# Two one-row tiles of their own for the streamed conditioning rows, in place of the eighth 4 KB tile

## The chip, the cores and the metric

The kernel runs on one core of one Trainium2 chip. The metric is the device time of one execution in microseconds (us). The profile comes from one execution; its engines are PE (TensorE matmuls), PEld (TensorE weight loads, which overlap PE), DVE (VectorE), ACT (ScalarE), POOL (GpSimd) and SP (SyncE, which here only issues DMAs). L301 means line 301 of the kernel's file.

## What is computed

One layer of an encoder on x of 1024 tokens by 1024 channels, all in float32, conditioned on one vector c of 1024 entries:

```python
c_act = silu(c)
mod = c_act @ w_ada + b_ada                       # 6 x 1024 conditioning values
sh1, sc1, gt1, sh2, sc2, gt2 = split(mod, 6)
h = rms_norm(x, g_norm1) * (1 + sc1) + sh1
qa, ka, va, qb, kb, vb, gates = split(h @ w_in, ...)
o_a = neighbourhood_attention(norm(qa), norm(ka), va, rpb)          # 8 heads of 64
o_b = merge of 3 dilated window attentions on norm+rotary(qb, kb), vb   # 3 x 4 heads of 64
gate_a, gate_b = split(sigmoid(gates + b_gate))
x = x + gt1 * ((gate_a * (o_a @ w_proj_a) + gate_b * (o_b @ w_proj_b)) @ w_o)
h2 = rms_norm(x, g_norm2) * (1 + sc2) + sh2
a, up = split(h2 @ w_ffn_in)
x = x + gt2 * ((silu(a) * up) @ w_ffn_out)
```

sc1 and sh1 are needed at the very start. The other four, 4096 values, are first read after the attention, and it is their computation that the change touches.

## The kernel before, in words

**Precision.** Every matmul operand is split into a high and a low part (whi and wlo, made by `wsplit`, L118 on ACT and L119 on POOL or DVE), and each product is three matmuls.

**Stages.** First h is made (to about 48 us). Then a loop `for n in range(6, 92)` runs ten attention units `u` (two heads each) of eight token tiles `t`: the projection of the current unit (`proj_chunk`, L312, eight chunks per n), the normalisation of its result (`proj_post`, L326 to L366, the small tiles ss, ry, rv, rz and qn), the turning of q and k (`qk_turns`, L377, L399 to L402), and the attention of the unit before it (scores L476 or L543, softmax L490 to L494 or L553 to L555, turns L502 or L568, products with v L517 or L588). After u = 9 the loop goes on with the gates (`gate_pre`, L712). Then come the rest of the gates (`gate_prod`, L731), the merge, the output projection, and the feed-forward layer, which a fast block scheme runs as seven products in place of eight.

**The order of the work.** The instructions of PE are issued in the order in which the code is written. For ACT, DVE, POOL and SP that holds to the end of the first stage; from then on a list scheduler orders them when the kernel is built, from the priority of the code's order and from durations and transfer times that it assumes. On the chip each engine's list is fixed and runs in order: an instruction that waits holds up all behind it on its engine. SP is one such list, for loads and stores alike. A tile that takes a buffer can be written only when the tile that had the buffer has been read for the last time, and the scheduler places its load accordingly.

**The conditioning rows.** The 4096 values are made on DVE, beside the loop over n. A step `ada_step()` (one in each n from 8 on with t < 7, and from u = 9 on in every n; 64 in all) takes one [128, 512] block of w_ada, multiplies it by one column of c_act and adds it to the accumulator acc (L299 for the first of eight, L301 for the others). After eight steps PE sums acc over the partitions (L271, in `ada_row`), DVE adds the bias (L275) and SP stores the row. acc has one buffer. The blocks (tile name wa in the profile) come in pairs: one DMA (L283) loads two of them, 512 KB, into a big tile; at each even step the pair of that step and the next pair are asked for.

**The big tiles.** The tag `big` has eight buffers (`NBIG = 8`) of 4 KB in each partition. Besides the pairs of conditioning blocks it holds: in the first stage the landing tiles (seven, `NLAND = 7`, read by L789), then the v of each unit (loaded at L362 to L366 for units 2 to 9), two tiles (hi, lo) for each of the eight mixes of h (`t_piece`, tile tp, L751 to L761), two tables of biases (rb, L424) for each of the last four units, the accumulators of the dilated merge (oacc), the gates' results (gsig, L718, L719) and two tiles for each of two weight mixes (w1m, L766 to L772). When the loop is over, this pool is released and its place taken by the tiles of the next stage, among them tg (L1051), which L731 reads.

Of the kernel before, what the change touches and what calls it, by code (L numbers as in the profile page):

```python
# [10 lines left out]
F32 = mybir.dt.float32  # L11
# [32 lines left out]
def hybrid_layer(ctx: ExitStack, tc: tile.TileContext, x, colp, wada1, wada2, bada2, wqkv, wg, wpa, wpb,  # L44
                 wo, w1, w2, hgain, ropeg, rope, rbias, bmask, g2r, out):
    nc = tc.nc

    def pool(name, side, **kw):
        return tc.alloc_tile_pool(name=name, bufs=1, side=side, reuse_waits="tile", **kw)
# [93 lines left out]
    ap_ = pool("attn", "right")  # L143
# [2 lines left out]
    nc.vector.memset(c32, 0.0)  # L146
    nc.vector.tensor_copy(c32[:, :, 0], cact)

    NBIG, NLAND = 8, 7

    def big(name, shape=None, dtype=F32):
        return ap_.tile(shape or wide, dtype, tag="big", bufs=NBIG, name=name)
# [1 line left out]
    yT = [ap_.tile([128, 4, S], F32, tag="qk", bufs=2, name="yT") for _ in range(2)]  # L154
    land = [big("land") for _ in range(NLAND)]
    for tag, n, bufs in (("bm", 512, 1), ("p", 512, 4), ("qn", 256, 7), ("rtab", 512, 1), ("acc2", 512, 1), ("pT", 512, 4),
                         ("stg", 512, 3), ("vs", 128, 2), ("ra", 64, 2), ("rb", 64, 2)):
        ap_.tile([128, n], F32, tag=tag, bufs=bufs, name="place")
    seq = [0]

# [106 lines left out]
    ada_acc = {}  # L267

    def ada_row(c):
        pm = bank("t")  # L270
        nc.tensor.matmul(pm[0:1, :], ones, ada_acc[c], start=True, stop=True)  # L271
        row = wp.tile([1, 512], F32, tag="raw", bufs=NRAW, name="row")
        br = wp.tile([1, 512], F32, tag="raw", bufs=NRAW, name="brow")
        nc.sync.dma_start(br, bada2[:, c * 512:(c + 1) * 512])
        nc.vector.tensor_add(row, pm[0:1, :], br)  # L275
        nc.sync.dma_start(mod_d[c * 512:(c + 1) * 512].rearrange("(o n) -> o n", o=1), row)

    def ada_load(i):

        if i < 64 and i not in ada_acc.setdefault("w", {}):  # L280
            c, kk = divmod(i, 8)
            ada_acc["w"][i] = big("wa2", [128, 2, 512])
            nc.sync.dma_start(ada_acc["w"][i], wada2[c, :, kk:kk + 2, :])  # L283

    def ada_step():
        i = ada_state["i"]
        ada_state["i"] += 1
        c, kk = divmod(i, 8)
        if kk == 0 and c > 0:
            ada_row(c - 1)  # L290
        if i >= 64:
            return
        if kk % 2 == 0:
            ada_load(i)
            ada_load(i + 2)
        wa = ada_acc["w"][i - kk % 2][:, kk % 2, :]
        if kk == 0:
            ada_acc[c] = ap_.tile([128, 512], F32, tag="acc2", bufs=1, name="acc2")
            nc.vector.tensor_scalar(ada_acc[c], wa, cact[:, 0:1], None, op0=ALU.mult)  # L299
        else:  # L300
            nc.vector.scalar_tensor_tensor(ada_acc[c], wa, cact[:, kk:kk + 1], ada_acc[c],  # L301
                                           op0=ALU.mult, op1=ALU.add)
# [619 lines left out]
    for n in range(6, 92):  # L922
# [78 lines left out]
        if n >= 8 and (t != 7 or u > 8) and ada_state["i"] < 65:  # L1001
            ada_step()
# [663 lines left out]
```

## Time and profile before

| | before |
|---|---|
| median of 3 runs | 1508.83 us (1507.0 to 1510.0) |
| the profiled execution: its time / its span | 1508.52 us / 1506.7 us |
| busy share of the span: PE, DVE, ACT, POOL | 99%, 72%, 44%, 36% |
| DMA packets, bytes | 150637, 241.65 MB |

The span goes from the first instruction to the last. Busy shares are averages over stages that differ; since PE is busy nearly throughout, what counts is where it is not. A row of the waits names an instruction, what it waited for, the total in us, how often, and the longest wait. A row of the timeline begins with the start in us and the duration in us, then engine, line, operation, tiles (out<-in), shapes and count; in square brackets stands the idle time of the engine just before and what ended it. SPq marks DMA issues by SP.

### The profile page before, as it was taken

How to read it: one execution, taken by the hardware profiler on the slowest of the kernel's cores; microseconds unless marked ns; L12 is line 12 of the kernel's file. 1: busy time of each engine (PE TensorE's matmuls, PEld its weight loads, DVE VectorE, ACT ScalarE, POOL GpSimd, SP SyncE). 2: the span in 40 equal slices, each digit the busy share in tenths (PEclk: the TensorE clock that was granted, in tenths of full speed). 3: DMA queues.
4: the chain of work that ended last, by engine and by line, in shares of the span. 5: the costliest groups of instructions: out<-in, count | busy, mean ns of one | idle time of the engine just before them, and what ended most of it. 6: DMA issues, size and time to landing. Idle time of an engine off the chain costs nothing. (4 is left out here: it accounts for less than half of the span.)

```text
span 1506.7 us, 24201 instructions
## 1 busy us (share of the span) xinstructions
PE 1485.7 (99%) x8156; PEld 1265.1 (84%) x8156; DVE 1090.2 (72%) x2265; ACT 668.2 (44%) x1691; POOL 535.1 (36%) x540
## 2 busy tenths in 40 slices
PE   9999999999999999999999999999999999999998
PEld 7998989998888877788888888888888888887886
DVE  6867767767889845367675597788767777599468
ACT  5555655555645554246432354233223323354442
POOL 0432332321100040002352301676767776104464
PEclk9999999999999999999999999999999999999999
DMA  9625445645245164824553225345433334898342
GB/s 373 236 85 179 144 132 162 196 139 166 61 131 168 45 197 143 327 85 128 161 195 137 90 90 181 126 127 181 155 125 109 108 106 144 278 372 281 98 153 100
DMA packets 150637, 241.65 MB, mean 160 GB/s; under 512 B 26464, under 2 KB 69088, under 8 KB 149744
## 3 DMA queue, kind: packets, MB, share of 16 engines
q1 hardware_dynamic: 131936, 226.45, 45.7%
q10 hardware_dynamic: 18576, 13.64, 2.8%
q8 instruction: 65, 1.06, 0.3%
q14 instruction: 60, 0.49, 0.1%
HBM read 179.89 MB, written 60.15 MB: 159 GB/s over the span
## 5 line engine op out<-in xcount | busy, mean ns | idle before, releaser
L119 POOL TENSOR_TENSOR wlo<-raw,whi 128x512 fp32r<-128x512 f32 (+2 forms) x133 | 172.9, 1314 | 461.7 <-ACT whi L118 287.0
L118 ACT ACTIVATE whi<-raw 128x512 fp32r<-128x512 f32 (+1 forms) x348 | 203.6, 599 | 252.4 <-PE ps_s L1501 42.3
L312 PE MATMUL ps_d<-whi,hT 128*128 128x384 f32 x1152 | 310.8, 341 | 0.0
L119 DVE TENSOR_TENSOR wlo<-raw,whi 128x512 fp32r<-128x512 f32 (+1 forms) x215 | 183.6, 867 | 76.8 <-ACT whi L118 72.4
L312 PEld LDWEIGHTS ps_d<-whi,hT 128*128 128x128 f32 x1152 | 209.9, 188 | 5.2 <-ACT vs L350 3.5
L312 PE MATMUL ps_d<-wlo,hT 128*128 128x384 f32 x576 | 193.6, 336 | 2.9 <-DVE wlo L119 2.7
L312 PEld LDWEIGHTS ps_d<-wlo,hT 128*128 128x128 f32 x576 | 108.7, 189 | 4.0 <-DVE wlo L119 3.4
L118 ACT ACTIVATE whi<-ws 128x512 fp32r<-128x512 f32 x65 | 40.8, 628 | 126.9 <-DVE ws L1348 79.8
L1281 POOL TENSOR_TENSOR e<-e,c 128x512 f32<-128x512 f32 x44 | 68.9, 1565 | 59.2 <-DVE c L1411 35.0
L342 POOL TENSOR_TENSOR ra<-qn,rtab 128x64 f32<-128x64 f32 x48 | 16.3, 340 | 156.7 <-DVE qn L335 105.8
L119 POOL TENSOR_TENSOR wlo<-m,whi 128x512 fp32r<-128x512 f32 x35 | 51.4, 1479 | 54.5 <-ACT whi L118 54.5
L1279 ACT ACTIVATE e<-e 128x512 f32<-128x512 f32 x44 | 27.5, 631 | 95.1 <-DVE e L1414 66.4
L555 ACT ACTIVATE P<-P,st 128x256 f32<-128x256 f32 (+2 forms) x100 | 45.8, 460 | 41.4 <-DVE st L553 41.3
L712 PE MATMUL ps_d<-hT,whi 128*128 128x512 f32 x192 | 60.6, 397 | 0.0
L1331 PE MATMUL ps_v<-h2T,whi 128*128 128x512 f32 x192 | 59.2, 389 | 0.0
L1331 PE MATMUL ps_s<-h2T,whi 128*128 128x512 f32 x192 | 59.1, 389 | 0.0
L129 ACT ACTIVATE ry<-ss,eps 128x4 f32<-128x4 f32 (+1 forms) x88 | 26.2, 298 | 70.1 <-DVE ss L333 56.7
L1331 PE MATMUL ps_d<-h2T,whi 128*128 128x512 f32 x184 | 56.8, 390 | 0.0
L491 ACT ACTIVATE P<-P,sx 128x384 f32<-128x384 f32 (+1 forms) x64 | 37.1, 580 | 43.6 <-DVE sx L490 43.4
L119 DVE TENSOR_TENSOR wlo<-ws,whi 128x512 fp32r<-128x512 f32 x45 | 49.7, 1105 | 8.0 <-ACT whi L118 7.8
L1280 DVE TENSOR_TENSOR e<-e 128x512 f32<-128x512 f32 x44 | 42.5, 973 | 17.8 <-ACT e L1279 17.7
L301 DVE SCALAR_TENSOR_TENSOR acc<-wa,cact,acc 128x512 f32<-128x512 f32 x56 | 42.6, 762 | 16.8 <-DMA wa<-in_wada_dram 16.5
(445 smaller groups left out, 3956.8 us busy)
## 6 DMA issues: line engine op xcount, KB each, us to landing
raw<-in_w_dram SPq DMA_DIRECT2D x139, 256.0 KB
ga_d<-e SPq DMA_DIRECT2D x77, 256.0 KB
raw<-ga_d SPq DMA_DIRECT2D x77, 256.0 KB
wa<-in_wada_dram SPq DMA_DIRECT2D x32, 512.0 KB
raw<-in_wqkv_dram SPq DMA_DIRECT2D x80, 192.0 KB
m<-in_w_dram SPq DMA_DIRECT2D x44, 256.0 KB
raw<-in_wg_dram SPq DMA_DIRECT2D x42, 256.0 KB
xt<-in_x_dram SPq DMA_DIRECT2D x16, 512.0 KB
```

The costliest lines, as they stand in the source:

```text
L118: nc.scalar.activation(hi[:, :n], r, AF.Copy)
L119: (eng or nc.gpsimd).tensor_sub(lo[:, :n], r, fview(hi[:, :n]))
L129: nc.scalar.activation(y, ss, AF.Ln, scale=1.0 / n, bias=eps)
L301: nc.vector.scalar_tensor_tensor(ada_acc[c], wa, cact[:, kk:kk + 1], ada_acc[c], op0=ALU.mult, op1=ALU.add)
L312: nc.tensor.matmul(pd[:, :384], tok(a, k, t), U.w[k][b][:, :384], start=(k == 0 and i == 0), stop=(k == KT - 1 and i == 2))
L491: nc.scalar.activation(P[:nq, :nk], P[:nq, :nk], AF.Exp, scale=-1.0, bias=nm, accum_out=sm)
L555: nc.scalar.activation(C.P[h][:nq, c], C.P[h][:nq, c], AF.Exp, scale=-1.0, bias=nm, accum_out=sm)
L712: nc.tensor.matmul(st["p"], gw[i, br][j][a][:, kk * 128:(kk + 1) * 128], hT[b][:, k, hs], start=(k == 0 and q == 0), stop=(k == 7 and q == 2))
L1279: nc.scalar.activation(sg, a, AF.Sigmoid)
L1280: nc.vector.tensor_mul(sg, sg, a)
L1281: nc.gpsimd.tensor_mul(sg, sg, up)
L1331: nc.tensor.matmul(pb, w[p][:, k * 128:(k + 1) * 128], b[q][:, k], start=(k == 0 and i == 0), stop=(k == 3 and i == 2))
```

## The change

The big tag has seven buffers in place of eight. A new tag `wa` has two buffers of one block each, [128, 512] or 2 KB in each partition, so that the pool's size stays the same (8 x 4 KB against 7 x 4 KB and 2 x 2 KB). Each step asks for its own block and that of the next step; a DMA loads one block, 256 KB. There are 64 such loads in place of 32, for the same 16.8 MB. The accumulation itself (L299, L301) and the order of PE are as before.

```diff
-    NBIG, NLAND = 8, 7
+    NBIG, NLAND = 7, 7
...
-                         ("stg", 512, 3), ("vs", 128, 2), ("ra", 64, 2), ("rb", 64, 2)):
+                         ("stg", 512, 3), ("wa", 512, 2), ("vs", 128, 2), ("ra", 64, 2), ("rb", 64, 2)):
         ap_.tile([128, n], F32, tag=tag, bufs=bufs, name="place")
...
         if i < 64 and i not in ada_acc.setdefault("w", {}):
             c, kk = divmod(i, 8)
-            ada_acc["w"][i] = big("wa2", [128, 2, 512])
-            nc.sync.dma_start(ada_acc["w"][i], wada2[c, :, kk:kk + 2, :])
+            ada_acc["w"][i] = ap_.tile([128, 512], F32, tag="wa", bufs=2, name="wa2")
+            nc.sync.dma_start(ada_acc["w"][i], wada2[c, :, kk, :])
...
-        if kk % 2 == 0:
-            ada_load(i)
-            ada_load(i + 2)
-        wa = ada_acc["w"][i - kk % 2][:, kk % 2, :]
+        ada_load(i)
+        ada_load(i + 1)
+        wa = ada_acc["w"][i]
```

## The prediction

> **What bounds the kernel now.** I read the page first: the busy times, then the costliest groups.
>
> ```profile
> span 1506.7 us, 24201 instructions
> PE 1485.7 (99%) x8156; PEld 1265.1 (84%) x8156; DVE 1090.2 (72%) x2265; ACT 668.2 (44%) x1691; POOL 535.1 (36%) x540
> ```
>
> PE is idle for 1506.7 - 1485.7 = 21.0 us in all. The change adds and removes no matmul, so unless the clock moves, 21 us is all that any edit of this kind can give back. How much of it lies in the stretch where the conditioning blocks are read? The line that accumulates them tells the stretch, and the sums over that stretch and the one behind it tell the idle time:
>
> ```profile
> L301 DVE SCALAR_TENSOR_TENSOR acc<-wa,cact,acc x56: 729/747/1590, 62.9 to 487.7; 128x512 f32<-128x512 f32 x56
> L283 SPq DMA_DIRECT2D wa<-in_wada_dram x32: 327/423/799, 54.6 to 477.2; - x32
> 55.00:525.00 470.00, 459.69 (x3276) 419.66 (x3275) 362.88 (x1195) 271.57 (x956) 110.10 (x237) 1.00 0.43 135
> 525.00:620.00 95.00, 95.00 (x564) 74.11 (x563) 42.75 (x118) 40.23 (x101) 18.05 (x14) 1.00 0.60 183
> ```
>
> Of the last two rows the first number behind the comma is PE: idle for 470.00 - 459.69 = 10.3 us in the attention stretch, and not at all from 525 to 620. DVE is busy for 362.88 of 470 there, 77%, so it is the engine that PE can be late behind. The waits of PE in that same stretch, longest first:
>
> ```profile
> PE ps_d L312 <- DVE wlo L119: 2.7, 1, 2.7
> PE ps_t L672 <- DVE PT L506: 1.4, 2, 1.0
> PE ps_v L377 <- POOL qn L345: 1.3, 1, 1.3
> PE ps_v L377 <- DVE rz L132: 1.2, 1, 1.2
> PE ps_t L502 <- DVE row L275: 1.1, 1, 1.1
> PE ps_s L476 <- DVE qk L402: 0.9, 1, 0.9
> ```
>
> And those of DVE:
>
> ```profile
> DVE rz L132 <- ACT ry L131: 18.6, 32, 1.5
> DVE ss L333 <- ACT sq L330: 18.4, 23, 2.2
> DVE acc L301 <- DMA wa<-in_wada_dram: 16.5, 8, 4.4
> ...
> DVE tp L753 <- DMA tp<-h_d: 7.9, 5, 2.0
> ```
>
> The six rows of PE make 8.6 of its 10.3 us, and five of them name DVE. On DVE the accumulation waited 16.5 us for its blocks, in 8 waits, mean 2.06 us: its longest wait for any DMA, and in an in-order queue the softmax and normalisation behind it stand too. These two lists are the case; the timeline has to say how far they belong together.
>
> **Part 1, the load's buffer and its date.** Taken away: 32 loads of 512 KB into big tiles. Added: 64 of 256 KB into tiles that nothing else uses. The timeline around four waits, each followed by the PE wait behind it, and the late loads themselves:
>
> ```profile
> 81.66 0.75 DVE L301 SCALAR_TENSOR_TENSOR acc<-wa,cact,acc 128x512 f32<-128x512 f32 x1 [1.47 <-DMA wa<-in_wada_dram]
> 86.14 0.44 PE L377 MATMUL ps_v<-ident,qn 128*128 128x128 f32 x2 [1.22 <-DVE rz L132]
> ...
> 135.50 0.58 SPq L283 DMA_DIRECT2D wa<-in_wada_dram  x1
> 140.89 0.75 DVE L301 SCALAR_TENSOR_TENSOR acc<-wa,cact,acc 128x512 f32<-128x512 f32 x1 [1.53 <-DMA wa<-in_wada_dram]
> 146.00 0.44 PE L377 MATMUL ps_v<-ident,qn 128*128 128x128 f32 x2 [1.30 <-POOL qn L345]
> ...
> 361.38 1.59 SPq L283 DMA_DIRECT2D wa<-in_wada_dram  x3
> 367.13 0.75 DVE L301 SCALAR_TENSOR_TENSOR acc<-wa,cact,acc 128x512 f32<-128x512 f32 x1 [2.78 <-DMA wa<-in_wada_dram]
> 369.02 0.50 PE L476 MATMUL ps_s<-qk 64*128 64x256 f32 x4 [0.95 <-DVE qk L402]
> ...
> 412.86 7.46 SPq L283 DMA_DIRECT2D wa<-in_wada_dram  x3
> 418.31 0.75 DVE L301 SCALAR_TENSOR_TENSOR acc<-wa,cact,acc 128x512 f32<-128x512 f32 x1 [3.41 <-DMA wa<-in_wada_dram]
> 421.14 0.66 PE L672 MATMUL ps_t<-ident,fb 128*128 128x128 f32 x4 [0.98 <-DVE PT L506]
> ```
>
> In each of the four, DVE stood for 1.47 to 3.41 us, always longer than the PE wait that follows, 0.95 to 1.30 us, and what PE then waited for is work that DVE does behind the accumulation (rz; qn by way of POOL; qk; PT). Were DVE earlier by its wait, each of the four would be gone: 1.22 + 1.30 + 0.95 + 0.98 = 4.45 us. The other four of the eight waits, 16.5 - 1.47 - 1.53 - 2.78 - 3.41 = 7.3 us, have no PE wait of that size behind them, and I let them give nothing.
>
> Does the change take these waits away? At 361.38 and 412.86 three loads go out in a row, six steps' worth. Nothing was asked for in between, and that is how loads look that stood in line for a big tile (v, rb and oacc take theirs there). With tiles of their own they go out when the block two steps before has been used. From the second block to the 64th one step takes (487.7 - 62.9) / 62 = 6.9 us; a 512 KB load took 140.89 - 135.50 = 5.39 us from issue to use, and half the bytes should take no longer, so a block asked for one step ahead is there in time on average. Bound above: all four PE waits go, -4.45 us. Bound below: as many of the 64 loads wait as now do of the 32, rival C. I take the upper end, since the late loads in a row are what stands ahead of the two longer waits, and these go with the shared buffers.
>
> **Part 2, twice the issues.** 32 more issues at a median of 423 ns are 13.5 us on SP over some 425 us. SP's own waits in the stretch:
>
> ```profile
> SPq L111 <- POOL wlo L119: 66.9, 16, 16.8
> SPq L617 <- ACT qn L331: 18.1, 1, 18.1
> ```
>
> SP waits 66.9 us for the buffers of the weight loads alone; issues laid ahead of such a wait take their time from it, so 13.5 us fit in and I take 0. If a pair of issues fell just ahead of a late weight load, PE would lose 2 x 0.42 = 0.84 us, which goes into the range. What is queued behind a block's load on SP is v, tp, rb and the weights; a block load waits only for DVE's accumulation two steps before.
>
> **Part 3, bytes.** Unchanged, 32 x 512 KB = 16.8 MB. The DMA share in the stretch is 0.43, so this is off the path: 0. The first two blocks no longer need a landing tile's buffer and may be loaded earlier than 54.6 us, into the busy start; 2 x 256 KB at the 135 GB/s of that row would be 3.9 us of transfer, hidden or at worst set against weight loads. I take 0.
>
> **Part 4, seven big tiles.** The first unit's v now waits for a landing tile instead of taking the eighth buffer; the landing tiles are read for the last time from 18.4 to 46.9 us, and the fifth of eight readings frees the first, before the first v is written: 0. In the loop the conditioning pairs held two or three of eight, so the others lose nothing. Only behind 488 us, when no block is left, is it truly one tile fewer:
>
> ```profile
> 557.00 0.87 SPq L766 DMA_DIRECT2D w1m<-in_w_dram  x2
> 563.40 0.91 SPq L766 DMA_DIRECT2D w1m<-in_w_dram  x2
> ...
> 603.88 0.41 SPq L772 DMA_DIRECT2D w_d<-w1m  x1
> 618.55 3.38 SPq L1051 DMA_DIRECT2D tg<-t_d  x6
> ```
>
> and the one wait of PE for such a load, behind 620:
>
> ```profile
> PE ps_t L731 <- DMA tg<-t_d: 0.6, 1, 0.6
> ```
>
> PE is never idle up to 620 and the last weight mix is stored 618.55 - 603.88 = 14.7 us before the tiles that take this place are loaded: 0, with rival D for when the cover is gone.
>
> **Sum.** -4.45 + 0 + 0 + 0 = -4.45 us. The profiled execution took 1508.52 us, its span 1506.7 and 1.8 us around it; it would take 1504.1. The median of the runs shown is 0.3 us higher, 1508.83, so I say 1504.4 us, 0.3% less. About 0.2%, 3 us, is what can be told from no change here.
>
> **Rivals.**
>
> **B, no difference.** DVE's waits go or shrink, but the scheduler lays out all of ACT, DVE and SP anew, and other small waits of the same kind come in. For it: half of DVE's wait for the blocks, 7.3 of 16.5 us, costs PE nothing now, and the PE waits are single events of 1 us, the sort that a new order deals out afresh. Against it: four of them follow on one cause. It gives 1508.8, within 3 us.
>
> **C, the step ahead is too short; slower.** The mechanism: with two one-block buffers no load can run further ahead, whereas a pair asked for two steps ahead has up to four blocks in hand. Every block then comes just in time, and each one that a busy SP sends late stops DVE in order. If the share that waits stays at 8 of 32 loads with the same mean, 64 loads make 16 x 2.06 = 33 us of DVE waits. Of today's 16.5 us, 4.45 came through to PE, 27%; of 33 us, 8.9: 4.45 more than now, 1513.3. It decides from the point where the blocks' waits on DVE pass 16.5 us. For it: SP once stands 18.1 us for one store (the L617 row), longer than two steps. Against it: 5.39 us of load against a step of 6.9. [...]
>
> **D, one big tile fewer behind 488 us; slower.** Each weight mix takes two tiles; the second half of the first already came 6.4 us behind the first half (563.40 after 557.00). If the second mix is stored 20 us later, it passes the 14.7 us of slack and the loads for L731 come 5.3 us later; PE waits for these already (0.6 us), so it pays in full: 1514.1. Against it: from 525 to 620 PE never stood, so this part has cover, and only the gates' results and the weight mixes are new there.
>
> **E, the long wait goes too.** The longest PE wait is not from a block, but any new order may dissolve it:
>
> ```profile
> 215.70 0.45 PE L312 MATMUL ps_d<-wlo,hT 128*128 128x384 f32 x1 [2.67 <-DVE wlo L119]
> 216.00:220.00 4.00, 4.00 (x16) 3.56 (x16) 2.37 (x11) 1.72 (x7) 1.63 (x7) 0.59 0.28 82
> ```
>
> After 2.67 us of idle PE the granted clock was 0.59 over the next 4 us (0.41 x 4 = 1.64 us lost), so it costs 4.31 us; the time would be 1508.8 - 4.45 - 4.31 = 1500.1. [...] A new order can also make such a wait; that lies in C's price.
>
> **How the numbers follow.** My forecast A (1504.4, its own range 1502 to 1506) 0.36; E 0.08; B 0.28; C 0.20; D 0.08. Faster by over 0.2%: A and E, 0.44. Within: 0.28. Slower: C and D, 0.28. The range reaches from a little beyond E to a little beyond D, with the 0.84 us of part 2: 1499 to 1515.
>
> **What would show it.** Part 1 is right if the blocks' total wait on DVE falls below some 6 us and the PE rows for qk, PT, qn and rz (L476, L672, L377) shrink; if the loads stand singly, a step apart, and not in threes. C shows as a total above 16.5 us with PE waits behind it. D shows as a PE wait of L731 for tg above 0.6 us and w1m stored later than 603.88. B shows as PE idle near 10 us in 55 to 525 with other names. The prediction is wrong if PE's waits come from elsewhere than DVE's queue, or the new order loses more than the blocks give.

## The result and the profile after

The changed kernel is slower: a median of 1518.83 us (1516.87 to 1519.83, 4 runs) against 1508.2 us for the kernel before on the same chip, a ratio of 1.0068 with a 95% interval of 1.0050 to 1.0085. The forecast was 1504.4 us, and the result lies beyond the range's upper end of 1515. The profiled execution took 1516.87 us.

In the changed file the lines behind the block loads (L283) have numbers lower by one: the accumulation L301 is now L300, the projection L312 is L311, and so on; in the experiments they are moved by a line or two again. First the span and the engines' busy time:

```profile
span 1514.8 us, 24275 instructions
PE 1489.7 (98%) x8156; PEld 1268.0 (84%) x8156; DVE 1090.0 (72%) x2265; ACT 669.8 (44%) x1691; POOL 537.8 (36%) x540
```

PE has the same 8156 matmuls and 8 us more of span. The windows say in which stage; the first number behind the comma is PE. Before, first stage (its other two rows stand in the prediction):

```profile
0.00:55.00 55.00, 51.71 (x419) 45.36 (x420) 39.14 (x101) 30.28 (x65) 4.58 (x12) 1.00 0.94 364
```

and after:

```profile
0.00:55.00 55.00, 49.72 (x396) 42.80 (x396) 37.87 (x98) 29.37 (x63) 3.49 (x11) 0.97 0.97 375
55.00:525.00 470.00, 456.86 (x3241) 417.40 (x3242) 360.50 (x1178) 268.04 (x941) 112.60 (x239) 0.99 0.44 133
525.00:620.00 95.00, 95.00 (x584) 74.57 (x583) 45.31 (x136) 42.46 (x115) 18.06 (x14) 1.00 0.51 154
```

PE's idle time grew by 51.71 - 49.72 = 2.0 us in the first stage and from 10.3 to 13.1 us in the attention stretch; the granted clock is below full in both (0.97 and 0.99). From 525 to 620 PE is never idle, as before. The waits of PE in the attention stretch, longest first, and DVE's wait for the blocks:

```profile
PE ps_d L311 <- DVE wlo L119: 3.0, 1, 3.0
PE ps_v L376 <- POOL qn L344: 2.6, 3, 1.2
PE ps_d L311 <- ACT vs L349: 2.4, 1, 2.4
PE ps_v L376 <- DVE rz L132: 1.6, 1, 1.6
PE ps_t L501 <- DVE P L493: 1.3, 2, 0.9
...
DVE acc L300 <- DMA wa<-in_wada_dram: 15.1, 18, 2.0
```

The blocks' total wait hardly moved (16.5 before), but it is now 18 waits of 0.84 us where it was 8 of 2.06 us: the two loads asked for singly come late more often, each a little. From the issue of a load to the first accumulation that reads it, the median counted from the traces fell from 8.9 us to 5.2 us. PE's list has other names on it than before.

Since PE's matmuls are the same and in the same order, the k-th matmul of one trace can be set against the k-th of the other, and every step of the difference has a place. By that account (us that the changed kernel is later; gains at their time in the trace of before, losses at theirs in the trace of after):

| place | step | what it is |
|---|---|---|
| up to 40 | +4.05 | a landing tile 1.53 late, a granted clock of 0.50 for 3.41 us, rowk 0.70 late |
| 86.1, 146.0, 369.0, 421.1 | -4.70 | the four waits of the forecast are gone (-1.42, -1.05, -1.08, -1.15) |
| 215.7 | -4.20 | the wlo wait of rival E and its half clock (a granted clock of 0.59 from 216 to 220 us) are gone |
| 404.2 | -1.36 | the wait for row is gone |
| 197.0, 311.4, 318.9, 418.9 | +5.5 | new waits for POOL's qn (twice), POOL's wlo, DVE's P |
| 291.8 | +3.9 | new wait for ACT's vs, with a half clock behind it (0.66 from 292 to 297 us) |
| 367.4 | +4.5 | new wait for DVE's wlo, with a half clock behind it (0.66 from 367 to 372 us) |
| 427.5 | +1.7 | new wait for DVE's rz |

The gains come to 10.3 us, more than was forecast; the losses to 19.6; with small steps the end is 8.09 us later. Of the losses some 7.7 us (311.4, 367.4, 427.5) lie just behind late blocks, 4.05 at the start, and some 8 us at places with no late block just ahead of them. The second trace of the change (below) ends 5.99 us behind that of before, mostly by the same waits. How one of the losses comes about is in the timeline, DVE with PE's wait at the end:

```profile
356.82 1.29 DVE L300 SCALAR_TENSOR_TENSOR acc<-wa,cact,acc 128x512 f32<-128x512 f32 x1 [2.05 <-DMA wa<-in_wada_dram]
...
358.14 0.75 DVE L300 SCALAR_TENSOR_TENSOR acc<-wa,cact,acc 128x512 f32<-128x512 f32 x1
...
361.60 0.75 DVE L300 SCALAR_TENSOR_TENSOR acc<-wa,cact,acc 128x512 f32<-128x512 f32 x1 [0.60 <-DMA wa<-in_wada_dram]
...
364.36 1.14 DVE L300 SCALAR_TENSOR_TENSOR acc<-wa,cact,acc 128x512 f32<-128x512 f32 x1
365.43 1.21 DVE L334 TENSOR_TENSOR qn<-qn,ry 128x256 f32<-128x256 f32 x1
...
366.77 0.54 DVE L119 TENSOR_TENSOR wlo<-raw,whi 128x384 fp32r<-128x384 f32 x1
...
367.36 0.44 PE L311 MATMUL ps_d<-wlo,hT 128*128 128x384 f32 x1 [2.98 <-DVE wlo L119]
```

```profile
362.76 0.28 ACT L633 ACTIVATE fe<-fe 128x96 f32<-128x96 f32 x1 [3.12 <-DVE fe L632]
```

Ahead of the wlo that PE needs, DVE does four accumulations within 9 us, 1.29 + 0.75 + 0.75 + 1.14 = 3.93 us, and stands 2.65 us for two of their blocks. ACT, which makes the whi parts, stood for DVE too (the second fence). Its last whi before this wlo was done at 365.00, and DVE was not idle from then to 366.77: at the end it is DVE's own list, and not a late weight load, that holds the wlo up. On SP the same stretch shows the loads:

```profile
358.14 0.33 SPq L283 DMA_DIRECT2D wa<-in_wada_dram  x1
358.56 0.41 SPq L111 DMA_DIRECT2D raw<-in_wqkv_dram  x1
359.07 0.41 SPq L283 DMA_DIRECT2D wa<-in_wada_dram  x1
359.53 1.38 SPq L111 DMA_DIRECT2D raw<-in_wqkv_dram  x3
```

Blocks and weights alternate. Before, the three block loads at 361.38 (in the prediction) stood behind the unit's nine weight loads. That they stood there for want of a big tile, as the prediction reads them, is not shown: the trace has no wait of these issues for a tile.

### The profile page after: what moved, and what is told of

Its sections match the earlier page's. It is cut to its first block, busy times and chain, and to the rows that moved or that the text cites. A ratio compares the mean times of both kernels' runs of the same rounds, so it can differ in the third digit from the quotient of the medians.

```text
span 1514.8 us, 24275 instructions
## 1 busy us (share of the span) xinstructions
PE 1489.7 (98%) x8156; PEld 1268.0 (84%) x8156; DVE 1090.0 (72%) x2265; ACT 669.8 (44%) x1691; POOL 537.8 (36%) x540
## 4 chain that ended last, share of the span: by engine, by line
PE 81%; DVE 8%; DMA 7%; issue 2%; ACT 1%; POOL 1%; SPq 0%; ACTq 0%; DVEq 0%; POOLq 0%
PE ps_d L311 13%; PE ps_v L1330 7%; PE ps_d L1330 7%; PE ps_s L1330 7%; PE ps_t L1330 6%; PE ps_d L711 4%; DMA wa<-in_wada_dram 3%; PE ps_s L1500 3%; PE ps_d L1500 3%; PE ps_s L1265 2%; PE ps_d L1265 2%; PE ps_v L1500 2%; PE ps_t L1500 2%; DVE wlo L119 2%; PE ps_v L1265 1%
## 5 line engine op out<-in xcount | busy, mean ns | idle before, releaser
L311 PE MATMUL ps_d<-whi,hT 128*128 128x384 f32 x1152 | 311.9, 342 | 2.4 <-ACT vs L349 2.4
L311 PEld LDWEIGHTS ps_d<-whi,hT 128*128 128x128 f32 x1152 | 210.8, 189 | 7.8 <-ACT vs L349 6.8
L311 PE MATMUL ps_d<-wlo,hT 128*128 128x384 f32 x576 | 194.3, 337 | 3.8 <-DVE wlo L119 3.0
L311 PEld LDWEIGHTS ps_d<-wlo,hT 128*128 128x128 f32 x576 | 109.2, 190 | 5.3 <-DVE wlo L119 3.3
L300 DVE SCALAR_TENSOR_TENSOR acc<-wa,cact,acc 128x512 f32<-128x512 f32 x56 | 42.9, 766 | 15.3 <-DMA wa<-in_wada_dram 15.1
```

What stands on the lines that cost most here:

```text
L311: nc.tensor.matmul(pd[:, :384], tok(a, k, t), U.w[k][b][:, :384], start=(k == 0 and i == 0), stop=(k == KT - 1 and i == 2))
```

## The experiments

Four theories stood against each other after the result: that the early block loads cost the start (S below); that the blocks' loads, now free to go at any time, come just in time and stop DVE (W); that they stand in the way of the weights on SP (Q); and that the change only dealt another hand of the scheduler's order (O). Each ratio is to the kernel before on the same chip, with its 95% interval. `keep_in_program_order` forbids the scheduler to place an instruction ahead of anything written before it for the same engine.

**The start: the first two loads held back.**

```diff
+            ld = nc.sync.dma_start(ada_acc["w"][i], wada2[c, :, kk, :])
+            if i < 2:
+                tc.keep_in_program_order(ld)
```

> The changed kernel, but the loads of the first two blocks are pinned behind what SP has been given before them in the code's order, so that no block is loaded in the first stage. Theory S (the blocks that now go out at 21.4, 21.8, 34.6 and 38.6 us take the queue and the bandwidth from the landing tiles, which costs PE 4.05 us by 40 us): that loss goes, 1518.8 - 4.05 = 1514.8 us, and PE waits for no landing tile (1.5 us now). Theory O (the remaining loss is the scheduler's new order of DVE, ACT and SP, not one cause): some 1514.8 too, but with PE waits at other places again, give or take 4. Theory W (blocks come just in time and stop DVE): 1518.8 less the start, with DVE's wait for blocks still 15 us. If none of S: 1518.8.

1514.67 us, ratio 1.0061 (1.0046 to 1.0076). In the changed kernel the first loads lie between the landing tiles; held back they go out at 66.70 us. The fences show the changed kernel's loads and then the run with the two held back:

```profile
21.36 0.80 SPq L283 DMA_DIRECT2D wa<-in_wada_dram  x2
23.12 0.33 SPq L178 DMA_DIRECT2D land<-in_wada_dram  x1
```

```profile
0.00:55.00 55.00, 50.95 (x416) 44.62 (x417) 38.93 (x101) 30.37 (x65) 4.62 (x12) 1.00 0.92 361
DVE acc L302 <- DMA wa<-in_wada_dram: 18.0, 21, 2.6
```

The first stage gets 1.2 of its 2.0 us back, and the granted clock in it is 1.00; the waits for blocks stay. Not only loads went into the first stage: in the changed kernel two accumulations run there at 31.49 and 33.29 us, so the scheduler also puts work written later into that stage. Both kernels once more, side by side on one chip, the unchanged file of the change first:

> The changed kernel itself, so that the run with two pinned loads has it beside it on the same chip. Theory S: 4 us above that run. If the start is worth nothing: the same as that run. Either way some 1.0068 of the kernel before.

1517.61 us, ratio 1.0070 (1.0052 to 1.0087). Its trace is 4.01 us behind by 41 us, again with a late landing tile, a granted clock of 0.97 from 0 to 55 us and rowk; the loss came in both traces.

> The changed kernel with the first two loads pinned, as before (1.0061 of the kernel before, then on another chip than the changed kernel). Theory S: 4 us below the changed kernel beside it, 1.004 of the kernel before. If the start is worth nothing: the same as the changed kernel.

1516.29 us, ratio 1.0055 (1.0037 to 1.0073). By the medians the start is worth 1.3 us, not the 4 us of theory S, and the intervals overlap; the trace shows the loss, the time does not separate it. Most of the slowdown is elsewhere, since 1.0055 is left with the loads held.

**All block loads in the order of the code.** The same line of code, held for every i.

```diff
+            tc.keep_in_program_order(nc.sync.dma_start(ada_acc["w"][i], wada2[c, :, kk, :]))
```

> The changed kernel with every load of a block pinned in the code's order on SP: a block is asked for where its step before stands in the code, never earlier. S: start loss gone, 1514.8 at most. W: loads come later than the scheduler would place them, so DVE waits more for blocks than 15.1 us, and the time is above that of the run with two pinned loads: 1516 or more. O: no order of these two is foretold; 1510 to 1518.

1523.65 us, ratio 1.0119 (1.0102 to 1.0136), slower still.

```profile
DVE acc L300 <- DMA wa<-in_wada_dram: 24.7, 28, 2.9
PE ps_d L311 <- DVE wlo L119: 7.5, 5, 2.5
```

Held loads mean more waits on DVE, and PE waits for wlo 7.5 us in all. More waits for blocks and more time go together, as W foretold; that loads which go too early are the trouble is not borne out.

**The block loads on ACT's queue** (first two held), so that they neither delay the weights on SP nor wait behind them.

```diff
+            ld = nc.scalar.dma_start(ada_acc["w"][i], wada2[c, :, kk, :])
```

> The changed kernel with the first two loads pinned, and all block loads issued by ACT in place of SP. Theory Q (blocks stand ahead of the weight loads in SP's order): PE's 3.4 us wait for wlo near 364 goes, 1.002 or less of the kernel before. Theory W: DVE still waits for each block (15 us or more, as ACT is busy too), 1.0055 as with SP.

1522.68 us, ratio 1.0106 (1.0091 to 1.0122). Q foretold 1.002 or less. PE's wait for wlo at the change of unit did shrink, from 3.40 to 1.36 us (at 369), but DVE has more waits for blocks than with SP, and the time is worse. So taking the block loads off SP gains nothing in sum, which speaks against Q as the main cause; why the loads come later from ACT's queue, behind ACT's own work perhaps, was not traced.

```profile
DVE acc L302 <- DMA wa<-in_wada_dram: 20.6, 24, 3.5
DVE acc L300 <- DMA wa<-in_wada_dram: 1.3, 1, 1.3
```

**No block loads.** Only the first two blocks are loaded; 62 loads are left out and the 64 accumulations read these two again and again.

> The changed kernel with only the first two blocks loaded (pinned as in the first run) and used for all 64 steps: the other 62 loads and their waits are left out, the accumulations stay. W: DVE's 15.1 us of waits for blocks are gone, and with them the PE waits that follow them (about 1.6 at 427, 1.2 at 311, 2 of the 3.0 at 367): some 5 us below the run with two pinned loads, 1510. O: the same as that run within 4 us, other waits in other places, although no block is waited for.

1507.4 us, ratio 1.0010 (0.9999 to 1.0022). That is 7.3 us below the run with two loads held, where W foretold some 5 and O no difference beyond 4. No wait for a block is left, and yet the kernel only comes back to where it was, not below. PE is idle for 470.00 - 460.65 = 9.35 us in the attention stretch, by waits of the known kind:

```profile
55.00:525.00 470.00, 460.65 (x3300) 420.31 (x3300) 364.75 (x1202) 273.60 (x958) 112.35 (x237) 1.00 0.33 101
PE ps_v L379 <- POOL qn L347: 2.8, 3, 1.1
PE ps_d L314 <- DVE wlo L119: 2.7, 2, 1.4
```

The loads, that is the waits for blocks, the traffic and the order that the scheduler makes around them, are therefore worth 1.0061 - 1.0010, about 0.5%; the three are not separated by this run. What makes PE wait in this kernel cannot be a block's load. What is left is the order of DVE's work, and the place of the accumulations in it is tried below. In this kernel 42 of the 63 steps from one accumulation's start to the next are under 2 us, counted from the trace; in the kernel before 39 are.

**The parts of the change alone.** Seven big tiles, the pairs as before:

```diff
-    NBIG, NLAND = 8, 7
+    NBIG, NLAND = 7, 7
```

> The kernel before with seven big tiles in place of eight and nothing else: pairs of blocks still go into big tiles, 512 KB each. Theory G (the eighth big tile is what is missing): pairs, v, rb and oacc stand in line longer, DVE's wait for blocks grows over 16.5 us, slower than before by 3 us or more, 1511 or above. If G is nothing: 1508.2, within 3 us. S says no loss at the start, since the pairs wait for landing tiles as before.

1507.44 us, ratio 1.0005 (0.9990 to 1.0019), waits for blocks 14.2 us in 7. Eight big tiles and pairs, but each pair loaded by two DMAs of 256 KB:

```diff
+            for z in range(2):
+                nc.sync.dma_start(ada_acc["w"][i][:, z, :], wada2[c, :, kk + z, :])
```

> The kernel before with each pair of blocks loaded into its big tile by two DMAs of 256 KB in place of one of 512 KB: as many loads and of the same size as in the changed kernel, but with the big tiles' buffers and their depth of two pairs. If number and size of the loads cost the time: 1.004 or more of the kernel before, with more than 8 waits of DVE for blocks. If it is the place and depth of the buffers (W or Q): 1.000, within 0.002.

1509.18 us, ratio 1.0018 (1.0005 to 1.0031), 15.8 us in 8. The missing tile makes none of the slowdown. Twice the loads, with the new order that comes with them, go with 0.18% of the 0.68%, just clear of none.

**Own tiles, but for pairs.** Six big tiles and two tiles of 4 KB that only the pairs use; one DMA of 512 KB for a pair, the first two pairs held.

> Six big tiles and two own tiles of one pair each (the seventh landing tile takes one of them), pairs loaded by one DMA of 512 KB as before, the first two pairs pinned; accumulations not pinned. Own buffers without the one-block size. If it is the own buffer as such that brings the loads too early among the weight loads: 1.004 or more, many waits of DVE for blocks. If it is the depth of two single blocks: four blocks in hand, few waits, 1.000 or less.

1510.72 us, ratio 1.0028 (1.0017 to 1.0040), 8.2 us in 7 waits. With twice the data in hand, buffers of its own halve the waits for blocks, as the forecast thought, and still nothing is gained: PE is idle for 9.9 us in the attention stretch. Neither forecast came true as it stood. Here two big tiles are missing, not one, and what six of them alone cost was not run; nor were eight with buffers of their own.

**The accumulations held in the order of the code**, nothing else of the kernel's work changed. Added to the change with the first two loads held:

```diff
+            tc.keep_in_program_order(nc.vector.tensor_scalar(ada_acc[c], wa, cact[:, 0:1], None, op0=ALU.mult))
         else:
+            tc.keep_in_program_order(nc.vector.scalar_tensor_tensor(ada_acc[c], wa, ...))
```

> The changed kernel with the first two loads pinned and every accumulation of a block pinned in the code's order on DVE, so that it is no longer laid into the first free place after its block's supposed landing, but a step after its block was asked for. Theory W (what costs is DVE standing for blocks that were placed just in time): DVE's waits for blocks fall to 2 us or less, and the time to that of the run without loads, 1.001 of the kernel before, 1508. Theory Q (what costs is that block loads go out ahead of the weight loads on SP): the blocks are still loaded early, PE's 3.4 us wait for wlo at the change of unit near 364 stays, 1.003 to 1.006.

1498.27 us, ratio 0.9943 (0.9927 to 0.9958): 1.1% less than with the accumulations free, and some 10 us below what either theory foretold. Every wait for a block is gone, and these are all that is left of PE's waits over 0.15 us in the attention stretch:

```profile
55.00:525.00 470.00, 468.34 (x3344) 427.42 (x3343) 370.10 (x1215) 276.36 (x967) 116.38 (x238) 1.00 0.45 138
PE ps_t L673 <- DVE PT L507: 1.0, 2, 0.7
PE ps_t L271 <- DVE PT L507: 0.4, 1, 0.4
PE ps_t L673 <- ACT PT L509: 0.2, 1, 0.2
```

Holding the accumulations moves the loads too, since a block's tile comes free only after its accumulation: at that change of unit only two block loads go out among the weight loads (341.85 and 344.96 us), where the changed kernel has six. So this run alone does not part W from Q. The same on the change as it was, loads free:

> The changed kernel with every accumulation pinned in the code's order on DVE, and nothing else: the first two loads may go out in the first stage. Theory S: two blocks now go out ahead of landing tiles (not four, since the third waits for an accumulation that is pinned behind the first stage), so 1 to 2 us above the run with pinned loads, 0.995 to 0.996. If the start is worth nothing: 0.994.

1499.21 us, ratio 0.9955 (0.9943 to 0.9966). That is the number of theory S, but not its mechanism: this trace, with two block loads out at 21.16 us, is 1.5 us behind at 50 us, and that with the loads held is 3.3 us behind. And on the kernel before:

> The kernel before (eight big tiles, pairs of blocks) with every accumulation pinned in the code's order on DVE, and nothing else. If the early placing of the accumulations is the whole matter: DVE's 16.5 us of waits for blocks fall, and with them PE's waits, to the 0.994 of the changed kernel with pinned accumulations. If the pairs are late because they stand in line for a big tile: the waits for blocks stay in part, 0.997 to 1.001, and the change is then worth the difference.

1495.71 us, ratio 0.9928 (0.9916 to 0.9940), the fastest of all. No wait of DVE for a block, and PE idle for 0.72 us of 470:

```profile
55.00:525.00 470.00, 469.28 (x3362) 427.99 (x3361) 367.78 (x1215) 277.86 (x970) 119.07 (x238) 1.00 0.45 140
PE ps_t L271 <- DVE PT L506: 0.3, 1, 0.3
PE ps_t L672 <- ACT PT L508: 0.2, 1, 0.2
352.86 1.62 SPq L283 DMA_DIRECT2D wa<-in_wada_dram  x3
```

The last row matters: the loads still go out three in a row behind the unit's weights, at 352.86 us, as at 361.38 in the kernel before. Counted from the traces, none of the 32 block loads has changed its place in SP's order. What moved is the order on DVE, the accumulations above all and some of its other work with them, and the waits are gone. So this run, more than any other, shows what the early places cost.

What the accumulations do where the scheduler is free shows in the kernel before, around one of its PE waits:

```profile
398.66 0.49 DVE L299 TENSOR_SCALAR acc<-wa,cact 128x512 f32<-128x512 f32 x1
399.19 2.38 DVE L301 SCALAR_TENSOR_TENSOR acc<-wa,cact,acc 128x512 f32<-128x512 f32 x2
402.83 0.74 DVE L301 SCALAR_TENSOR_TENSOR acc<-wa,cact,acc 128x512 f32<-128x512 f32 x1
403.50 0.67 DVE L275 TENSOR_TENSOR row<-ps_t,brow 1x512 f32<-1x512 f32 x1
404.22 0.55 PE L502 MATMUL ps_t<-ident,P 128*128 128x128 f32 x3 [1.06 <-DVE row L275]
```

Four accumulations stand ahead of the row that frees the PSUM tile PE waits for; the sum they go into comes only at 471 us. The row starts 5.47 us behind PE's last matmul for it. With the accumulations held (the kernel before), that is 4.20 us; the row comes first and the next accumulations follow one by one:

```profile
392.94 0.67 DVE L275 TENSOR_TENSOR row<-ps_t,brow 1x512 f32<-1x512 f32 x1
393.54 0.47 DVE L299 TENSOR_SCALAR acc<-wa,cact 128x512 f32<-128x512 f32 x1
404.48 0.74 DVE L301 SCALAR_TENSOR_TENSOR acc<-wa,cact,acc 128x512 f32<-128x512 f32 x1
409.66 0.74 DVE L301 SCALAR_TENSOR_TENSOR acc<-wa,cact,acc 128x512 f32<-128x512 f32 x1
```

All together, in the order of the ratio (waits for blocks on DVE; steps between accumulations under 2 us, of 63; PE's idle time from 55 to 525 us):

| kernel | waits for blocks | steps < 2 us | PE idle | ratio |
|---|---|---|---|---|
| before, accumulations held | 0 | 1 | 0.7 us | 0.9928 |
| change, first loads and accumulations held | 0 | 1 | 1.7 | 0.9943 |
| change, accumulations held | 0 | 1 | 1.3 | 0.9955 |
| before | 16.5 us in 8 | 39 | 10.3 | 1 |
| seven big tiles, pairs | 14.2 in 7 | 38 | 8.7 | 1.0005 |
| change without 62 loads | 0 | 42 | 9.4 | 1.0010 |
| before, two DMAs for each pair | 15.8 in 8 | 38 | 11.7 | 1.0018 |
| six big tiles, own pairs | 8.2 in 7 | 35 | 9.9 | 1.0028 |
| change, first loads held | 18.0 in 21 | 23 | 14.9 | 1.0061 |
| change | 15.1 in 18 | 20 | 13.1 | 1.0068 |
| change, loads on ACT's queue | 21.9 in 25 | 25 | 17.9 | 1.0106 |
| change, all loads in code order | 24.7 in 28 | 14 | 16.9 | 1.0119 |

## Why the prediction was wrong

**Part 1, the step that failed.** Its first half held: the four named PE waits went, and gave 4.70 us where 4.45 were forecast. Its second half did not: "a block asked for one step ahead is there in time on average". It set 5.39 us of load against a mean step of 6.9 us. The mean hides bursts: the median of the 63 steps in the trace of before is 1.67 us, and 39 are under 2 us; after, the median is 2.24 us. With the accumulations held in the order of the code only one step is under 2 us, so the bursts come from the list scheduler, which seems to take an accumulation as soon as it believes the block to be there. No full step then lies between two accumulations, and with buffers that nothing else holds each block is used 5.2 us behind its request (median) where it was 8.9. The 18 loads that DVE waited for in the changed kernel took 2.75 to 5.60 us from issue to use, mean 4.17: longer than the median step. Before, one late pair made one wait and the second block of the pair was there; now each late block makes its own wait: 18 in place of 8, and the 16.5 us of waits became 15.1 at other places. The bound below in part 1, "rival C", was the right end of the two, and the result lies beyond it. The loads do go out singly for the most part, which was named as the sign of a right part 1; the sign came without the gain.

Two rows were misread on the way, both to the good of the forecast. The accumulation at 140.89 us is the first of the seventh pair, and the semaphore that ended its wait is that of the load issued at 133.69 us, not at 135.50:

```profile
133.69 0.56 SPq L283 DMA_DIRECT2D wa<-in_wada_dram  x1
```

So this load took 7.21 us and not 5.39, more than the mean step that it was set against; the eight loads that DVE waited for before took 5.34 us in the mean. And the row at 412.86 us merges three loads over 7.46 us: they went out at 412.86, 419.50 and 419.94 us, so the one behind the wait at 418.31 went out alone. Of the two longer waits, which the forecast put down to three late loads in a row, only that at 367.13 had such loads ahead of it, and with the accumulations held such loads cost nothing (352.86 above).

**Part 2.** Twice the issues as such: 1.0018 with two DMAs for each pair, just clear of nothing. How the time of a load issued by SP goes with its size is not settled here. By the loads that ended a wait, 256 KB took 4.17 us in the mean (18 loads, after) and 512 KB took 5.34 us (8 loads, before), a ratio of 0.78. By the few landings that the profile tells, medians of 2.8 us (8 of 64 loads, the change with first loads and accumulations held) and 5.1 us (3 of 32, the kernel before with accumulations held), it is 0.55.

**Part 3.** The early loads were seen ("may be loaded earlier, into the busy start") with 3.9 us as their worst case, and taken as 0. That figure used the 135 GB/s of the attention stretch; the first stage moved 364 GB/s. And not two blocks but four went out before 40 us, with two accumulations. Twice the trace of the change is some 4.0 us behind by 41 us, and with the loads held the first stage has most of its PE time again in two traces (50.95 and 51.33 us busy). But the kernel with loads and accumulations both held was also 3.3 us behind by 50 us, the one with early loads and held accumulations 1.5 us, and the times don't separate them. What the early loads alone cost stays open, between 0 and 4 us.

**Part 4 and rival D.** Part 4 was right and D did not come: seven big tiles cost nothing (1.0005), PE is not idle from 525 to 620 us, and its wait for tg is 0.4 us where it was 0.6.

**Rival E** came true as a step, 4.20 us where 4.31 were put, but not as a case: new waits of the same sort came with it. **Rival B** was right in this, that a new order deals the small waits out anew (the larger new losses lie where PE waited 0.1 us or not at all before), and wrong that they even out. **Rival C** had the sign and 1513.3 us; but it was to decide where the blocks' waits pass 16.5 us, and they are 15.1. So its mechanism, blocks that come just in time, was the right one, with the wrong measure: the total did not grow, the number of waits did. In the runs with the accumulations free and blocks loaded, 7 or 8 waits go with ratios of 1.0000 to 1.0028, 15 to 21 with 1.0055 to 1.0070 (the repeated runs among them), 25 to 28 with over 1.01. That the number is the cause is not shown: within the middle group the run with the fewest waits, 15, has the highest ratio.

**What the prediction did not ask.** It took the accumulations' places on DVE as given and looked at their waits alone. Those places are what the time hangs on: holding them is worth 0.7% on the kernel before and 1.1% on the changed one. With them held the change still costs 0.2 to 0.3% more than the kernel before (0.9943 and 0.9955 against 0.9928; the intervals of the first overlap). Most of the change's loss goes with the block loads, as leaving them out shows (1.0061 to 1.0010). That step of 0.5% is larger than what a new order alone made elsewhere (1.0005 to 1.0028), but how much of it is DVE's waits, and how much the order of SP's list, is not fully separated; the eager places cost a further 0.7% (1.0010 to 0.9943), which the kernel before pays as well. Which of the new waits at 197, 291.8, 318.9 and 418.9 us, with no late block just ahead of them, comes from which move of the scheduler was not traced; they make some 8 of the 19.6 us.

## What to carry to other kernels

Work that is not urgent on an engine as busy as DVE is here (72% of the span) needs a place, not only a buffer: a list scheduler that puts it as early as its data may be there sets it ahead of urgent work and makes it come just in time for its loads. Hold it in the order of the code before touching buffers. And set a load's time against the distribution of the steps in the trace, not against their mean; and match each wait with its own load before taking a load's time from two rows that stand near each other.

## What the hardware showed that was not expected

Less than 3 us of idle PE had half the clock behind it. In the traces of before and after, up to the last matmul, the granted clock was 0.50 for 3.41 us at a time: from 216.7 us before, and from 29.8, 292.7 and 367.8 us after (these three starts lie 77.0 and 22.0 times 3.41 us apart). In the 3.41 us ahead of each, PE was idle for 2.38 us in the trace of before, and for 1.89, 2.40 and 2.98 us in that of after. The windows around the three, with the granted clock as third number from the end:

```profile
28.00:34.00 6.00, 4.47 (x25) 3.66 (x22) 3.43 (x9) 2.36 (x5) 0.00 (x0) 0.72 1.03 413
292.00:297.00 5.00, 5.00 (x36) 4.55 (x35) 4.15 (x12) 1.72 (x7) 3.16 (x2) 0.66 0.71 205
367.00:372.00 5.00, 4.64 (x22) 4.38 (x24) 4.40 (x21) 1.73 (x7) 0.00 (x0) 0.66 0.81 240
```

Half the clock for 3.41 us costs about 1.7 us, an estimate (0.50 x 3.41); with it the wait of 2.40 us at 291.8 came to 3.9. Not every longer wait had it. In the kernel with the first loads held a wait of 3.40 us had a granted clock of 1.00 from 363 to 369 us, around its end:

```profile
364.37 0.45 PE L313 MATMUL ps_d<-wlo,hT 128*128 128x384 f32 x1 [3.40 <-DVE wlo L119]
363.00:369.00 6.00, 4.63 (x37) 4.21 (x38) 5.56 (x25) 2.49 (x9) 0.36 (x1) 1.00 0.85 242
```

In the second trace of that same kernel the same wait, again 3.40 us, had half the clock behind it, 0.72 from 367 to 373 us:

```profile
367.73 0.69 PE L313 MATMUL ps_d<-wlo,hT 128*128 128x384 f32 x1 [3.40 <-DVE wlo L119]
367.00:373.00 6.00, 5.27 (x32) 4.85 (x33) 5.27 (x25) 1.91 (x8) 0.00 (x0) 0.72 0.85 252
```

So the length of the wait alone does not decide. What does stays open.
